# Where the weights and the activations of a two-layer trunk begin in a partition: multiples of 128 bytes for the one, 64 bytes past one for the other

## The chip, the core and the metric

The kernel runs on one core of a Trainium2 chip. The metric is the device time of one execution in microseconds, the median of several runs. The core has five engines that matter here: TensorE (PE in the profile; its weight loads are listed apart as PEld), VectorE (DVE), ScalarE (ACT), GpSimd (POOL) and SyncE (SP), which here only issues DMAs.

## The reference

Two layers of a hybrid trunk on 256 tokens of width 1024, all in 32-bit floats. A layer norms x, multiplies it with one wide input matrix, runs four branches of attention on the pieces, gates and adds their outputs, multiplies with an output matrix, and ends with an MLP with a squared ReLU:

```python
def hybrid_layer(x, ...):
    h = rms_norm(x, g_mix)
    (sb_q, sb_k, sb_v, gla_q, gla_k, gla_v, gla_lr, gla_r, dn_qkv, dn_a, dn_b, dn_gate,
     dil_q, dil_k, dil_v, gate_logits) = jnp.split(h @ w_in, IN_OFFSETS, axis=-1)
...
    gates = jax.nn.sigmoid(gate_logits.reshape(B, S, N_BRANCH, D_MODEL))
    merged = jnp.zeros_like(x)
    for n, o in enumerate((o_sb, o_gla, o_dn, o_dil)):
        merged = merged + gates[:, :, n] * (o.reshape(B, S, BRANCH_WIDTH) @ w_branch[n])
    x = x + merged @ w_out
    h = rms_norm(x, g_mlp)
    return x + jnp.square(jax.nn.relu(h @ w_mlp_in)) @ w_mlp_out
```

The four branches are stick-breaking attention, gated linear attention, a gated delta rule and dilated attention, four heads each. `w_in` is 1024 x 7448, `w_mlp_in` 1024 x 4096, `w_mlp_out` 4096 x 1024.

## The kernel before

All weights come as a stream of units of 128 x 2048 numbers, in the order in which they are used (`unit_list`): the pieces of `w_in`, each branch's gates and output matrix, `w_out` (`wo`), `w_mlp_in` (`mi`) and `w_mlp_out` (`mo`). A unit comes in two halves of 128 x 1024, each with one DMA into one of six `raw` buffers.

To keep the precision of 32 bits, every operand of a large product is split in two: a part that the engine's rounded 32-bit type (`float32r`) holds, and the rest. For weights ACT copies `raw` into `whi` and DVE subtracts, `wlo = raw - whi` (lines 247 and 248; five buffers each). Activations are split the same way: `ah`, `al` for the normed x, `oh`, `ol` for the output of a branch, `mh`, `ml` for the gated sum, `uh`, `ul` for the inside of the MLP. A large product is then three: high by high, high by low and low by high. A half of a unit is 24 of them.

Each of these is one weight load of 128 columns and one matmul that streams 256 columns. Mostly the weights are the loaded side and the activations the streamed one (`unit_F`, `units_out`); in the units whose result is wanted token by token (`unit_T`) the activations are loaded and the weights streamed. In the unit `mini` only 64 columns are loaded. All of them are issued by the helper at line 199.

Between the halves of units stands the small work of the branches, as threads that each go one step further at the end of a half; a table of pauses (`PAUSE`), written by hand, says how many halves lie between a step and the one that needs it on another engine. The order on each engine is the order in which the code issues.

Buffers of a partition are laid one behind the other, each at the next multiple of 32 bytes. A buffer whose size isn't a multiple of 128 bytes so shifts all that come after it: the constants `C` (1422 numbers), the parameters `PR` (2 x 433), `nea` (4) and the buffers `d6` (6 x 260) do.

Of the kernel before, what the change touches and what calls it, by code (L numbers as in the profile page):

```python
# [19 lines left out]
NL = 2  # L20
# [53 lines left out]
# columns of the packed parameters of a layer  # L74
P_GMIX, P_GMLP, P_CONV, P_DTB, P_ALOG, P_GLAB = 0, 8, 16, 40, 44, 48
P_GLAG, P_DNG, P_DILQ, P_DILK, P_LR2, NPAR = 49, 113, 177, 241, 305, 433
# columns of the constants
C_ID, C_NEGU, C_NEG1, C_UT, C_GT, C_STR, C_SBN, C_DIL = 0, 128, 256, 384, 512, 640, 768, 896
C_COS, C_SIN, C_SEL, C_S32, C_I32, C_H4, C_AB, NCON = 1280, 1312, 1344, 1346, 1378, 1410, 1414, 1422
LV = (1, 2, 4, 8, 16, 32, 64)  # L80

# [37 lines left out]
def lay_out(inp):  # L119
    a = {k: np.asarray(v) for k, v in inp.items()}  # L120
    w_in, w_br, w_out, w_mi, w_mo = (a[k] for k in ("w_in", "w_branch", "w_out", "w_mlp_in", "w_mlp_out"))
    W = np.zeros((len(UNITS), 128, 2048), np.float32)

    def kcols(w, c0, n=256):
        """[p][kt][column]"""
        return w[:, c0:c0 + n].reshape(8, 128, n).transpose(1, 0, 2).reshape(128, 8 * n)

    def fcols(w, c0):
        """[p][half of the columns][kt][column]"""
        return w[:, c0:c0 + 256].reshape(8, 128, 2, 128).transpose(1, 2, 0, 3).reshape(128, 2048)  # L130

    def krows(w, r0, halves=1):
        """[p][half of the columns][kt][column]"""
        n = 1024 // halves
        return w[r0:r0 + 256].reshape(2, 128, halves, n).transpose(1, 2, 0, 3).reshape(128, 2048)

    for n, (l, kind, arg) in enumerate(UNITS):
        if kind == "inF":
            W[n] = fcols(w_in[l], OFF[arg])
        elif kind == "inT":  # L140
            W[n] = kcols(w_in[l], OFF[arg])
        elif kind == "mini":
            m = np.zeros((1024, 32), np.float32)
            m[:, 0:8] = w_in[l][:, 2320:2328]
            m[:, 8:24] = w_in[l][:, 1280:1296]
            W[n][:, :256] = kcols(m, 0, 32)
        elif kind == "gate":
            W[n] = fcols(w_in[l], OFF["gates"] + arg[0] * 1024 + arg[1] * 256)
        elif kind == "br":
            W[n] = krows(w_br[l, arg], 0, 2)  # L150
        elif kind == "wo":
            W[n] = krows(w_out[l], arg * 256)
        elif kind == "mi":
            W[n] = fcols(w_mi[l], arg * 256)
        else:
            W[n] = krows(w_mo[l], arg * 256)
    P = np.zeros((NL, 128, NPAR), np.float32)
    for l in range(NL):
        P[l][:, P_GMIX:P_GMIX + 8] = a["norm_mix_g"][l].reshape(8, 128).T
        P[l][:, P_GMLP:P_GMLP + 8] = a["norm_mlp_g"][l].reshape(8, 128).T  # L160
        P[l][:, P_CONV:P_CONV + 24] = a["dn_conv_w"][l].reshape(6, 128, 4).transpose(1, 0, 2).reshape(128, 24)
        P[l][:, P_DTB:P_DTB + 4] = a["dn_dt_bias"][l][None]
        P[l][:, P_ALOG:P_ALOG + 4] = a["dn_a_log"][l][None]
        P[l][:, P_GLAB] = a["gla_b_lr"][l]
        P[l][:, P_GLAG:P_GLAG + 64] = a["gla_norm_g"][l][None]
        P[l][:, P_DNG:P_DNG + 64] = a["dn_norm_g"][l][None]
        P[l][:, P_DILQ:P_DILQ + 64] = a["dil_q_norm_g"][l][None]
        P[l][:, P_DILK:P_DILK + 64] = a["dil_k_norm_g"][l][None]
        for r in (8, 40):
            P[l][r:r + 16, P_LR2:P_LR2 + 128] = a["gla_w_lr2"][l]  # L170
    X = np.ascontiguousarray(a["x"].reshape(256, 8, 128).transpose(2, 1, 0).reshape(128, 2048))
    C, M = constants()
    return {"xin": X, "w": W, "par": P, "con": C, "msk": M}


@with_exitstack
def trunk(ctx: ExitStack, tc: tile.TileContext, xin, w, par, con, msk, out, dbg=None, nl=NL):
# [26 lines left out]
    # ---------------- constants and x  # L204
    C = cons.tile([128, NCON], F32, name="C")
    MK = cons.tile([128, 5 * 128], U8, name="MK")
    x = cons.tile([128, 8, 256], F32, name="x")
    PR = cons.tile([128, NL, NPAR], F32, name="PR")
# [18 lines left out]
    # ---------------- the stream of weights  # L227
# [22 lines left out]
    def split_upto(h):  # L250
        """h counts halves of units"""
        while state["split"] <= min(h, 2 * total - 1):
            k = state["split"]
            hi = wp.tile([128, 1024], F32R, name="whi", bufs=HALVES)
            lo = wp.tile([128, 1024], F32R, name="wlo", bufs=HALVES)
            splits[k] = (hi, lo)
            src = raws.pop(k)
            if wcols(k // 2) == 256:
                # both parts side by side
                src, both = r3(src[:, :128], 4), r3(hi[:, :256], 4)  # L260
                ACT.copy(both[:, :, 0:32], src)
                DVE.tensor_sub(both[:, :, 32:64], src, both[:, :, 0:32].bitcast(F32))
            elif k == 0:
                state["first"] = (src, hi, lo)
            else:
                n = 512 if k == 1 else 1024
                for c in range(0, 1024, n):
                    split_part(src, hi, lo, slice(c, c + n))
            state["split"] += 1
            dma_upto(k + RAW)  # L270
# [15 lines left out]
    nc.sync.dma_start(C[:, C_NEG1 + 128:], con[:, C_NEG1 + 128:])  # L286
# [4 lines left out]
    # ---------------- small helpers  # L291
    def rsqrt(v, n, name):
        """v: [128, n] in SBUF, > 0"""
# [7 lines left out]
    def pause(name):  # L301
        """slack between a step and the one that reads it on another engine, in halves of units"""
# [18 lines left out]
    def new_act():  # L321
        return (acts.tile([128, 8, 256], F32R, name="ah"), acts.tile([128, 8, 256], F32R, name="al"))

    class Norm:
        """x times the gain, feature-major and split; the root mean square is applied to what is made of it"""
# [28 lines left out]
        def rows(self):  # L354
            """1 / rms of each token, on every partition"""
# [9 lines left out]
        def scaled(self, t):  # L365
            """x over the root mean square"""
# [4 lines left out]
        def flip(self):  # L371
            """from here on what is made of it needs no scale"""
# [12 lines left out]
    def half(h, evac_first=False):  # L385
        """weights of half h of the current unit; the halves after it are begun"""
# [11 lines left out]
    def mmF(o, wh, wl, c, h, kts=8, new=False):  # L398
        """feature-major product: three passes; that over the operand split last comes last"""
# [8 lines left out]
    def unit_F(h, new=False):  # L408
        """yields after each half, then a bank [128, 2, 256], feature-major; new: h has only just been made"""
# [7 lines left out]
    def unit_T(h):  # L417
        """token-major, a bank [128, 2, 256]"""
# [12 lines left out]
    def unit_mini(h):  # L431
        """feature-major [64, 256]: by the high parts of the weights and, 32 rows on, by the low ones"""
# [14 lines left out]
    def units_out(h, units, nm):  # L447
        """feature-major products in four banks [128, 2, 256], added to x; the last unit goes by output"""
# [49 lines left out]
    # ---------------- one layer  # L498
    def layer(l, nm):
# [5 lines left out]
        with tc.tile_pool(name=f"mlp{l}", bufs=1) as mp:  # L505
            uh = mp.tile([128, 32, 256], F32R, name="uh")
            ul = mp.tile([128, 32, 256], F32R, name="ul")
# [22 lines left out]
    def mixing(l, pr, mp, nm):  # L530
# [7 lines left out]

        def split_pair(ps):
            pair = [mp.tile([128, 2, 256], F32R, name=n, bufs=2) for n in ("oh", "ol")]  # L540
# [3 lines left out]
        def to_feature(o, br, tag):  # L544
            """o: token-major [128, 2, 256] in SBUF -> split feature-major"""
# [7 lines left out]
        def head_rms(o, gs, br, tag, need=None):  # L553
            """o: [128, 2, 4, 64]; gs: silu of the gate times the gain"""
# [16 lines left out]
        # ---- gated delta rule: the gates and their decays  # L571
        def decay_chain():
            yield ("mini",)
            nea = sm.tile([128, 4], F32, name="nea")
# [24 lines left out]
            # rows and columns of the running sums of g  # L599
# [15 lines left out]
            got["E"] = E = T([6, 260], "d6", 3).rearrange("p a b -> p (a b)")[:, :1536].rearrange(  # L615
# [11 lines left out]
        # the products with the queries, and the values  # L627
# [33 lines left out]
        # ---- gated delta rule  # L661
        def dn_chain():
# [4 lines left out]
            pre = T([6, 260], "d6", 3)[:, :, :256]  # L667
# [38 lines left out]
            MT = T([6, 260], "d6", 3).rearrange("p a b -> p (a b)")[:, :1536].rearrange(  # L706
# [23 lines left out]
            # (I + M)^-1 transposed: blocks of 32 by substitution, all heads at once, then by doubling.  # L730
            # mc[j, (t, h), k]: the blocks of -M transposed
# [31 lines left out]
            def half_y(t, s):  # L763
                """levels 32 and 64: only the blocks below the diagonal"""
# [69 lines left out]
        # ---- stick breaking  # L834
# [54 lines left out]
        # ---- dilated  # L889
        def rope_chain():  # L890
            yield ("dil_q", "dil_k")
            qk = got["dil_qk"]                                  # [128, 16 (q/k, t, h), 64]
# [94 lines left out]
        # ---- gated linear attention  # L987
# [41 lines left out]
        def gla_chain():  # L1029
# [24 lines left out]
            # the diagonal and the pairs of level 1, a column of each for a head  # L1054
# [14 lines left out]
            # levels 16 to 2, two at a time; two heads at a time  # L1069
# [31 lines left out]
        # ---- threads of small work beside the weights  # L1101
        done = set()

        class Thread:
# [4 lines left out]
            def advance(self):  # L1109
                """one stage; False when it must wait or is over"""  # L1110
# [53 lines left out]
        cin = T([6, 260], "d6", 3)[:, :, :259]  # L1164
# [81 lines left out]
        def unit_br(n):  # L1246
# [9 lines left out]
            for fp in range(4):  # L1256
# [15 lines left out]
                if n == GLA:  # L1272
                    got["m"].append((mp.tile([128, 2, 256], F32R, name=f"mh{fp}", tag=("U", "T", "Y0", "Y1")[fp]),
                                     mp.tile([128, 2, 256], F32R, name=f"ml{fp}",
                                             tag=("Vs", "dlT0", "dlT1", "sbs")[fp])))
# [18 lines left out]
    with tc.tile_pool(name="boot", bufs=2) as bp:  # L1294
        # the tensor engine is brought to its full clock while the first loads are under way
# [42 lines left out]
```

## Time and profile before

| | |
|---|---|
| median of 3 runs | 933.5 us (933.41 to 936.74) |
| span of the profiled execution | 932.1 us |
| TensorE busy, matmuls and loads | 910.4 and 884.4 us |
| DVE, ACT, POOL busy | 630.8, 534.4, 143.8 us |
| weights and other data read | 147.5 MB, 159 GB/s over the span |

A matmul's time in the profile is that from its start to its modelled end; matmuls overlap, so the distance between the starts of two that follow each other is what the stream of products costs, and not the listed mean of one. A granted clock of 1 is the upper of TensorE's two levels, 2.4 GHz, and 0.5 the lower, 1.2 GHz.

### The profile page before, as it was taken

The page shows a single profiled execution, that of the slowest core. Times are in us where ns is not written, and L with a number is a line of the kernel's source. Part 1 is how long each engine was busy: PE and PEld are TensorE (multiplying, and loading weights), DVE is VectorE, ACT ScalarE, POOL GpSimd, SP SyncE. Part 2 cuts the span into 40 slices and gives each one's busy share as a digit, 9 for nine tenths or more (in the row PEclk, how much of TensorE's full clock was granted, in tenths as well). Part 3 has the DMA queues.
Part 4 walks back from the last instruction along what each step waited for, and adds up shares of the span by engine and source line. Part 5 has one row for each costly group of instructions (what it writes and reads, how often), then busy time and mean ns, then how long its engine had stood idle before and what let it go on. Part 6 is the DMA issues. An engine that isn't in the chain of part 4 may idle for free.

```text
span 932.1 us, 18924 instructions
## 1 busy us (share of the span) xinstructions
PE 910.4 (98%) x7678; PEld 884.4 (95%) x7678; DVE 630.8 (68%) x1242; ACT 534.4 (57%) x842; POOL 143.8 (15%) x148
## 2 busy tenths in 40 slices
PE   8999999999999999999989999999999999999998
PEld 6899999999998999999988999999999989999998
DVE  5959999429577676644489599984485867665442
ACT  5596758754554655543456876586545545654331
POOL 3524201113212000000042450013030120000000
PEclk7999999999999999999999999999999999999999
DMA  8544454433544556656444445444344535656551
GB/s 278 199 139 133 140 178 135 144 130 114 162 142 171 174 190 201 203 188 197 152 135 142 142 132 168 158 138 153 98 154 135 208 113 183 204 197 198 191 161 46
DMA packets 43430, 149.78 MB, mean 161 GB/s; under 512 B 4944, under 2 KB 7248, under 8 KB 43344
## 3 DMA queue, kind: packets, MB, share of 16 engines
q1 hardware_dynamic: 43056, 148.35, 48.8%
q8 instruction: 60, 0.98, 0.4%
q10 hardware_dynamic: 288, 0.23, 0.1%
q14 instruction: 26, 0.21, 0.1%
HBM read 147.51 MB, written 1.05 MB: 159 GB/s over the span
## 4 chain that ended last, share of the span: by engine, by line
PE 84%; DVE 8%; ACT 3%; POOL 2%; issue 1%; DMA 1%; SPq 0%; DVEq 0%; ACTq 0%
PE bg L199 55%; PE fa L199 14%; PE fb L199 14%; POOL s L369 2%; DVE al L339 2%; DVE wlo L248 2%; ACT whi L247 1%; DVE x L486 1%; DMA x<-xin 1%; POOL sbs L859 1%; DVE s L1082 0%; DVE ush L751 0%; DVE ush L749 0%; DVE s L1068 0%; PE fb L972 0%
## 5 line engine op out<-in xcount | busy, mean ns | idle before, releaser
L248 DVE TENSOR_TENSOR wlo<-raw,whi 128x1024 fp32r<-128x1024 f32 (+2 forms) x280 | 350.0, 1268 | 183.0 <-ACT whi L247 182.9
L247 ACT CAST whi<-raw 128x1024 fp32r<-128x1024 f32 (+2 forms) x280 | 283.8, 1034 | 117.9 <-PE bg L199 58.2
L199 PE MATMUL bg<-ah,whi 128*128 128x256 f32 x1232 | 315.2, 292 | 6.4 <-ACT ah L375 4.6
L199 PE MATMUL bg<-al,whi 128*128 128x256 f32 x1232 | 305.6, 289 | 6.2 <-DVE al L339 6.2
L199 PEld LDWEIGHTS bg<-ah,whi 128*128 128x128 f32 x1232 | 239.6, 194 | 13.3 <-ACT ah L375 6.6
L199 PEld LDWEIGHTS bg<-al,whi 128*128 128x128 f32 x1232 | 238.7, 196 | 7.6 <-DVE al L339 7.4
L199 PE MATMUL bg<-ah,wlo 128*128 128x256 f32 x1216 | 179.6, 286 | 1.5 <-DVE wlo L248 1.5
L199 PEld LDWEIGHTS bg<-ah,wlo 128*128 128x128 f32 x1216 | 162.5, 195 | 2.5 <-DVE wlo L248 2.5
L199 PE MATMUL fa<-uh,whi 128*128 128x256 f32 x256 | 70.4, 276 | 0.0
L199 PE MATMUL fa<-uh,wlo 128*128 128x256 f32 x256 | 70.4, 276 | 0.0
L199 PE MATMUL fa<-ul,whi 128*128 128x256 f32 x256 | 69.7, 276 | 0.0
L199 PE MATMUL fb<-uh,whi 128*128 128x256 f32 x224 | 61.6, 276 | 0.0
L199 PE MATMUL fb<-uh,wlo 128*128 128x256 f32 x224 | 61.6, 276 | 0.0
L199 PE MATMUL fb<-ul,whi 128*128 128x256 f32 x224 | 61.0, 276 | 0.0
L513 ACT ACTIVATE sq<-rl 128x512 f32<-128x512 f32 x32 | 20.2, 632 | 70.3 <-DVE rl L512 70.3
L445 DVE TENSOR_TENSOR ul<-sq,uh 128x512 fp32r<-128x512 f32 x32 | 22.2, 693 | 43.2 <-ACT uh L444 43.2
L1271 POOL TENSOR_TENSOR mg<-mg,gt 128x512 f32<-128x512 f32 x20 | 31.1, 1572 | 129.2 <-DVE gt L1270 129.2
L199 PEld LDWEIGHTS fa<-uh,whi 128*128 128x128 f32 x256 | 48.1, 188 | 0.0
L199 PEld LDWEIGHTS fa<-uh,wlo 128*128 128x128 f32 x256 | 48.1, 188 | 0.0
L199 PEld LDWEIGHTS fa<-ul,whi 128*128 128x128 f32 x256 | 47.6, 188 | 0.0
L199 PEld LDWEIGHTS fb<-uh,whi 128*128 128x128 f32 x224 | 42.1, 188 | 0.0
L199 PEld LDWEIGHTS fb<-uh,wlo 128*128 128x128 f32 x224 | 42.0, 188 | 0.0
(276 smaller groups left out, 1470.5 us busy)
## 6 DMA issues: line engine op xcount, KB each, us to landing
raw<-w SPq DMA_DIRECT2D x275, 512.0 KB, 4.3
x<-xin SPq DMA_DIRECT2D x3, 256.0 KB, 6.1
out_dram<-x SPq DMA_DIRECT2D x3, 256.0 KB, 2.1
C<-con SPq DMA_DIRECT2D x1, 519.0 KB, 6.9
raw<-w SPq DMA_DIRECT2D x4, 128.0 KB, 5.3
gt<-msk SPq DMA_DIRECT2D x2, 160.0 KB, 4.7
x<-xin SPq DMA_DIRECT2D x2, 128.0 KB, 2.8
raw<-w SPq DMA_DIRECT2D x4, 64.0 KB, 3.9
```

What stands on the lines that cost most here:

```text
L199: PE.matmul(o, l, r, start=start, stop=stop, skip_group_check=True)
L247: ACT.copy(hi[:, c], src[:, c])
L248: DVE.tensor_sub(lo[:, c], src[:, c], hi[:, c].bitcast(F32))
L339: DVE.scalar_tensor_tensor(self.h[1][:, kt, :], x[:, kt, :], self.g[:, kt:kt + 1], self.h[0][:, kt, :].bitcast(F32), op0=OP.mult, op1=OP.s ...
L369: POOL.tensor_tensor(t[:, kt, :], x[:, kt, :], self.R, op=OP.mult)
L445: DVE.tensor_sub(lo, src, hi.bitcast(F32))
L486: DVE.tensor_add(xs, pairs[fp], xs)
L513: ACT.activation(sq, rl, AF.Square)
L859: POOL.tensor_tensor(sp[:, :, c:c + 128], sp[:, :, c:c + 128], over(STR, 2), op=OP.mult)
L1271: (DVE if n == GLA and MADD[fp] else POOL).tensor_tensor(m, m, g, op=OP.add)
```

## The change

No instruction is added, removed or moved: on each engine the same instructions stand in the same order and wait for the same semaphores. Only addresses change. Buffers whose size is not a multiple of 128 bytes are widened to one (`whole`), and the activations' buffers are made 128 bytes longer and used from their 17th number on (`shifted`). So that all of it fits, the scratch at the start of each partition that is kept for DMAs with descriptors made by software shrinks from 16384 to 4096 bytes.

Where an operand begins in its partition, in bytes past a multiple of 128 (slices in a buffer are whole multiples of 512 bytes, so this holds for all of them):

| buffers | before | after |
|---|---|---|
| `raw`, `whi`, `wlo` (weights) | 96 | 0 |
| `ah`, `al` | 96 | 64 |
| `oh`, `ol` and `mh`, `ml` | 64 | 64 |
| `uh`, `ul` | 32 | 64 |
| constants `C` | 0 | 0 |
| `x`, `PR` | 64 | 0 |
| most tiles of the branches | 64, some 0, 32 or 96 | 0 |

The diff, without the comments that it also drops:

```diff
+def whole(n):
+
+    return -(-n // 32) * 32
+
+
+def shifted(tile, n, by=16):
+
+    return tile[:, by:by + n]
...
-    C = cons.tile([128, NCON], F32, name="C")
+
+    C = cons.tile([128, whole(NCON)], F32, name="C")
...
-    PR = cons.tile([128, NL, NPAR], F32, name="PR")
+    PR = cons.tile([128, whole(NL * NPAR)], F32, name="PR")[:, :NL * NPAR].rearrange("p (l c) -> p l c", l=NL)
...
-    nc.sync.dma_start(C[:, C_NEG1 + 128:], con[:, C_NEG1 + 128:])
+    nc.sync.dma_start(C[:, C_NEG1 + 128:NCON], con[:, C_NEG1 + 128:])
...
     def new_act():
-        return (acts.tile([128, 8, 256], F32R, name="ah"), acts.tile([128, 8, 256], F32R, name="al"))
+        return tuple(r3(shifted(acts.tile([128, 2080], F32R, name=n), 2048), 8) for n in ("ah", "al"))
...
-            uh = mp.tile([128, 32, 256], F32R, name="uh")
-            ul = mp.tile([128, 32, 256], F32R, name="ul")
+            uh, ul = (r3(shifted(mp.tile([128, 8224], F32R, name=n), 8192), 32) for n in ("uh", "ul"))
...
+        def d6():
+            return T([whole(6 * 260)], "d6", 3)
+
         def split_pair(ps):
-            pair = [mp.tile([128, 2, 256], F32R, name=n, bufs=2) for n in ("oh", "ol")]
+            pair = [r3(shifted(mp.tile([128, 544], F32R, name=n, bufs=2), 512), 2) for n in ("oh", "ol")]
...
-            nea = sm.tile([128, 4], F32, name="nea")
+            nea = sm.tile([128, 16], F32, name="nea")[:, 0:4]
...
-        cin = T([6, 260], "d6", 3)[:, :, :259]
+        cin = r3(d6()[:, :1560], 6)[:, :, :259]
...
-                    got["m"].append((mp.tile([128, 2, 256], F32R, name=f"mh{fp}", tag=("U", "T", "Y0", "Y1")[fp]),
-                                     mp.tile([128, 2, 256], F32R, name=f"ml{fp}",
-                                             tag=("Vs", "dlT0", "dlT1", "sbs")[fp])))
+                    got["m"].append(tuple(
+                        r3(shifted(mp.tile([128, 544], F32R, name=f"{n}{fp}", tag=tags[fp]), 512), 2)
+                        for n, tags in (("mh", ("U", "T", "Y0", "Y1")), ("ml", ("Vs", "dlT0", "dlT1", "sbs")))))
...
-    nc = _bacc.Bacc("TRN2", target_bir_lowering=False, num_devices=1)
+    nc = _bacc.Bacc("TRN2", target_bir_lowering=False, num_devices=1, dynamic_dma_scratch_size=4096)
```

The other three uses of `d6` (`E`, `MT` and `pre`) are rewritten in the same way as `cin`.

## Rows read from the trace of the kernel before

**Rows 1.** The page: span, and busy time, share and instructions of each engine.
```profile
span 932.1 us, 18924 instructions
PE 910.4 (98%) x7678; PEld 884.4 (95%) x7678; DVE 630.8 (68%) x1242; ACT 534.4 (57%) x842; POOL 143.8 (15%) x148
```
**Rows 2.** The page: granted TensorE clock in 40 slices, in tenths (9 is 90% up).
```profile
PEclk7999999999999999999999999999999999999999
```
**Rows 3.** Timeline of PE, first MLP product: start us, us, engine, line, operation, out<-in.
```profile
319.88 0.28 PE L199 MATMUL bg<-ah,whi 128*128 128x256 f32 x1
...
320.84 0.28 PE L199 MATMUL bg<-ah,whi 128*128 128x256 f32 x1
```
**Rows 4.** The chain that ended last, second MLP product: start us, us, what.
```profile
387.02 1.36 PE fb L199 x12
388.38 1.36 PE fa L199 x12
```
**Rows 5.** The same chain, product with `w_out`.
```profile
266.07 1.42 PE fa L199 x12
267.49 1.42 PE fb L199 x12
```
**Rows 6.** Groups of matmuls: count | busy us, mean ns of one | idle before.
```profile
L199 PE MATMUL bg<-ah,whi 128*128 128x256 f32 x1232 | 315.2, 292 | 6.4 <-ACT ah L375 4.6 <-ACT whi L247 1.8
L199 PE MATMUL bg<-al,whi 128*128 128x256 f32 x1232 | 305.6, 289 | 6.2 <-DVE al L339 6.2
...
L199 PE MATMUL bg<-ah,wlo 128*128 128x256 f32 x1216 | 179.6, 286 | 1.5 <-DVE wlo L248 1.5
...
L199 PE MATMUL bg<-oh,whi 128*128 128x256 f32 x128 | 35.3, 296 | 1.1 <-DVE gt L1270 1.1
...
L199 PE MATMUL bg<-whi,ah 128*128 128x256 f32 x224 | 32.7, 288 | 0.0
...
L199 PE MATMUL fa<-mh,whi 128*128 128x256 f32 x64 | 17.8, 282 | 0.0
```
**Rows 7.** Timeline of PE in the unit `mini`, loads of 64 columns.
```profile
26.86 0.28 PE L199 MATMUL bg<-ah,whi 128*64 128x256 f32 x1
...
28.00 0.28 PE L199 MATMUL bg<-ah,whi 128*64 128x256 f32 x1
```
**Rows 8.** Timeline of PEld: eight loads whose matmuls stream 4 columns.
```profile
195.29 0.97 PEld L199 LDWEIGHTS fb<-C,dlT 128*128 128x128 f32 x8
```
**Rows 9.** Groups of weight loads, 128 and 64 columns.
```profile
L199 PEld LDWEIGHTS fa<-C,Y 128*128 128x128 f32 x32 | 3.7, 192 | 0.0
...
L199 PEld LDWEIGHTS fa<-U,Y 64*64 64x64 f32 x32 | 2.2, 134 | 0.5
```
**Rows 10.** Busy us in stretches: PE, PEld, DVE, ACT, POOL, then clock, DMA, GB/s.
```profile
100.00:120.00 20.00, 19.89 (x170) 19.20 (x169) 19.07 (x70) 14.52 (x19) 0.00 (x0) 1.00 0.50 162
120.00:140.00 20.00, 20.00 (x157) 18.95 (x157) 18.39 (x78) 9.96 (x22) 0.00 (x0) 1.00 0.52 164
140.00:160.00 20.00, 20.00 (x171) 19.52 (x171) 19.63 (x91) 16.25 (x28) 3.36 (x4) 1.00 0.40 126
...
293.00:381.00 88.00, 88.00 (x724) 87.95 (x723) 57.49 (x65) 48.01 (x62) 0.00 (x0) 0.98 0.57 186
...
470.00:506.00 36.00, 31.64 (x218) 29.41 (x217) 30.13 (x47) 19.02 (x39) 15.89 (x15) 0.91 0.41 133
...
560.00:600.00 40.00, 39.98 (x326) 38.25 (x325) 37.48 (x145) 24.21 (x40) 0.00 (x0) 1.00 0.49 159
```
**Rows 11.** Groups: DVE's subtraction of 128x512 for `ul`.
```profile
L445 DVE TENSOR_TENSOR ul<-sq,uh 128x512 fp32r<-128x512 f32 x32 | 22.2, 693 | 43.2 <-ACT uh L444 43.2
```
**Rows 12.** The instructions of tile `ml`: min/median/max ns of one.
```profile
L1237 DVE TENSOR_TENSOR ml<-mg,mh x8: 675/688/693, 262.9 to 728.2; 128x512 fp32r<-128x512 f32 x8
```
**Rows 13.** Waits: who waited for whom, us in total, times, longest.
```profile
DVE wlo L248 <- ACT whi L247: 182.9, 139, 6.5
...
PE bg L199 <- DVE al L339: 6.2, 6, 1.0
```
**Rows 14.** The page's DMA queues: kind, packets, MB, share of 16 engines.
```profile
q1 hardware_dynamic: 43056, 148.35, 48.8%
q8 instruction: 60, 0.98, 0.4%
```

More of the change, by code (lines that the diff above doesn't have):

```diff
@@ L614, in decay_chain @@
             yield from pause("e10")
-            got["E"] = E = T([6, 260], "d6", 3).rearrange("p a b -> p (a b)")[:, :1536].rearrange(
+            got["E"] = E = d6()[:, :1536].rearrange(
                 "p (a h c) -> p a h c", a=3, h=4)
@@ L666, in dn_chain @@
             cw = pr[:, P_CONV:P_CONV + 24]
-            pre = T([6, 260], "d6", 3)[:, :, :256]
+            pre = r3(d6()[:, :1560], 6)[:, :, :256]
             for b in range(6):
@@ L705, in dn_chain @@
             yield from pause("d13")
-            MT = T([6, 260], "d6", 3).rearrange("p a b -> p (a b)")[:, :1536].rearrange(
+            MT = d6()[:, :1536].rearrange(
                 "p (a h c) -> p a h c", a=3, h=4)
```

## The prediction

> **What bounds the kernel now.** I read the busy line first. The matmul row of TensorE is busy 910.4 of 932.1 us, DVE 630.8, ACT 534.4 [rows 1], and the granted clock stands at its upper level nearly everywhere [rows 2]. A busy matmul row alone proves little, since matmuls overlap; so I looked at how far apart their starts are, in the timeline of TensorE. From here I call that distance the pitch. It should be the same for all the large products: each loads 128 columns and streams 256 columns, and 256 columns at 2.4 GHz take 106.7 ns. It is not the same:
>
> - activations `ah`, `al` against weights `whi`, `wlo`: eight steps from 319.88 to 320.84 us, 120 ns each [rows 3];
> - activations `uh`, `ul` against the same weights: twelve in 1.36 us, 113.3 ns [rows 4];
> - activations `mh`, `ml`: twelve in 1.42 us, 118.3 ns [rows 5].
>
> The clock is at its upper level in all three, the instruction is the same, the weights lie in the same buffers, and no wait stands between. What differs is where the activations begin. By the table of positions ahead, weights are at 96 (bytes past a multiple of 128, which I call the phase), `ah` and `al` at 96, `uh` and `ul` at 32, `mh`, `ml`, `oh`, `ol` at 64. So the distance between the phases is 0, 64 and 32 bytes, and the pitch is 120, 113.3 and 118.3 ns: it falls as the distance grows. My reading is that the weight load of the next matmul, which runs beside the streaming of this one, meets it in the memory when both are at one phase.
>
> The rest of the page says that the pitch is worth time: TensorE waits for almost nothing (the longest wait in total is 6.2 us, for `al`), while DVE waits 182.9 us in total for ACT [rows 13]. The next engine is DVE, close behind in parts of the attention stage: 19.07, 18.39 and 19.63 of 20 us, and 37.48 of 40 in the second layer [rows 10].
>
> **The change part by part.** No engine's instructions change in number, order or waits; only addresses do.
>
> *Products with `ah` and `al`.* Phases 96 and 96 become 64 and 0 (or 0 and 64 where the activation is the loaded side). The page counts 1232 + 1232 + 1216 with the weights loaded and 3 x 224 with the activations loaded [rows 6], 4352 in all; 32 of them load only 64 columns (the unit `mini`), which leaves 4320. The nearest row with a distance of 64 bytes is that of `uh`: 113.3 ns [rows 4]. 4320 x (120.0 - 113.3) = 28.9 us.
>
> *Products with `oh`, `ol`, `mh`, `ml`.* Distance 32 becomes 64. 3 x 128 with `oh`, `ol` and 2 x 3 x 64 with `mh`, `ml` [rows 6] make 768; 768 x (118.3 - 113.3) = 3.8 us.
>
> *Products with `uh`, `ul`.* Distance 64 stays; the phases go from 96 and 32 to 0 and 64. Sixteen units of two halves, eight columns of tiles, three products, two layers: 1536. By the distance alone they gain nothing.
>
> *Does beginning on a multiple of 64 bring more than the distance?* The trace has no pair of 0 and 64, so I bound it. From above: 113.3. From below: eight weight loads of 128 columns whose matmuls stream only 4 columns start (0.97 - 0.19) / 7 = 0.111 us apart, one of them taking 192 ns [rows 8, 9]. There the load alone sets the pace; a load of 64 columns takes 134 ns, so the columns are what it pays for. A product that must load 128 new columns each time will hardly go under 111.4 ns. The products of `mini`, which load half as many columns at phases 96 and 96, go at 1.14 us for ten steps, 114 ns [rows 7]: with half the load the collision is almost gone, and what is left is again about 113. I take 113.3, the row with the same distance, and keep 111.4 for the range: 1.9 x 6624 = 12.6 us more.
>
> The Trainium skill ("TensorE: Matmul & The Clock Gate", Part 2, step 1) speaks against the change: TensorE has two independent read ports into SBUF, and loading the next weights takes no read bandwidth from the running matmul. By that rule phases could not matter, and the time would stay at 933.5. This case's trace disagrees: 120 against 113.3 ns for one and the same instruction.
>
> *The small products* (transposes, chunks of the branches) get phase 0 on both sides in most cases, where many had 64 on both. Equal stays equal; a few transposes that meet the constants lose their distance, some 100 of them by about 10 ns at the most: 1 us, inside the bounds.
>
> *DVE, ACT and DMA.* Their operands move too. The same subtraction of 128x512 takes 693 ns with tiles at phase 32 and 688 with tiles at 64 [rows 11, 12], so a phase costs them nothing that I can see. The scratch that shrinks to 4096 bytes serves a kind of queue that this kernel has not: the page lists hardware queues and instruction queues only [rows 14]. Nothing.
>
> *What the gain meets.* 32.7 us disappear from TensorE only where it is the bound. In the first product of the MLP it surely is: 88 of 88 us busy, DVE 57.49 [rows 10]; 1536 of the 4320 products lie there and in its twin, 10.3 us. In the attention stage a stretch of 20 us with some 170 products shrinks by up to 1.1 us, while DVE has 0.93, 1.61 and 0.37 us to spare, and 2.52 in 40. So DVE stays just under the bound but for the stretch from 140 us, short by 0.8; twice, for two layers: 1.5 us. Where a layer begins, TensorE waits for the norm (31.64 of 36 us busy from 470 us [rows 10]); what its 218 products save there, 1.5 us, is mostly given back, and likewise at the start: 2.5 us. Together 4 us are lost.
>
> **Sum.** The profiled span is 932.1 us; the median of the runs is 933.5, 1.4 us more for what lies around the span. 933.5 - 28.9 - 3.8 + 4 = 904.8.
>
> **The rivals.**
>
> *Alignment counts as well.* The load alone sets the pace, 111.4 ns for all 6624 products. For it: the row of loads is at phase 64, on a multiple of 64, and all present large products have a side at 32 or 96. Against: in [rows 4] nothing shows what the last 2 ns are. 12.6 us more off TensorE, of which DVE takes back about a third: 896.
>
> *Only the streaming counts* and the load hides: 106.7 ns. For it: 256 columns need no more. Against: the row of loads, 111.4 [rows 8]. 6.6 x 6624 = 43.7 us more, a third given back: 876. The Trainium skill (the same page, "Back-to-back issue gap") gives 262 cycles for 256 columns, which is 109 ns; by it the sum would be an estimated 886. No product here goes at that pace.
>
> *DVE becomes the bound.* Of the gain, 2784 x 6.7 + 3.8 = 22.5 us lie in the attention stage, where each chain of small steps hands work between DVE, ACT and TensorE with slack counted in halves of weights, and these halves get shorter. If half of it is lost in waits of TensorE for DVE: 912 to 916. For it: 19.63 of 20 us. Against: DVE itself waits 182.9 us for ACT's copies, whose pace follows the buffers that TensorE frees.
>
> *The change does nothing to the pitch*: it hangs on something that goes with the stage, not on the phase (the banks written, the units' order). Against: `mh` and `uh` products have the same loop and differ. 933.5.
>
> *Slower: the phase of the streamed side decides, not the distance.* Streamed at 32 the pitch is 113.3, at 64 it is 118.3, at 96 it is 120. If 64 is simply a bad phase, `uh` and `ul` lose what they have now: 1536 x (118.3 - 113.3) = 7.7 us, and `ah` gains 4320 x 1.7 = 7.3; and if with a load at 0 all went at 120, the loss would be 1536 x 6.7 + 768 x 1.7 = 11.6 us: 945. It decides from a pitch of about 119 for `uh`. Against: where activations are loaded at 96 and weights streamed at 96, the pitch is that of equal phases too.
>
> **How the numbers follow.** 113.3 ns, 904.8 us: 0.50. 111.4 ns, 896: 0.22. 106.7 ns, 876: 0.05. DVE bound, 914: 0.12. No change: 0.07. Slower, 945: 0.04. The range from 887 to 917 takes in the first, second and fourth with some room on both sides; the third, fifth and sixth stay out. Faster by over 0.5% (about what a measurement of this kernel can tell from no change): 0.50 + 0.22 + 0.05 + 0.12 = 0.89; within: 0.07; slower: 0.04.
>
> **What would show it.** In the timeline of after, products with `ah` 113 ns apart (eight steps in 0.91 us, not 0.96), twelve `mh` products in 1.36 us, `uh` unchanged at 1.36. Each MLP's first product shorter by 5.1 us. DVE's busy time as before, its waits for ACT shorter, TensorE's waits for `wlo` and the chains longer by a few us. The forecast is wrong if `ah` stays at 120, if `uh` moves by more than 2 ns, or if waits of TensorE grow by over 10 us.

## The result

The changed kernel takes 927.0 us where the kernel before took 933.7 in the same runs (medians of 12 runs each). The ratio is 0.9929, with an interval from 0.9913 to 0.9946: some 0.7% faster. The forecast was 904.8 us and its range ended at 887; the time lies 10 us above the upper end, 917.

The page after, span, TensorE's and the other engines' busy time, and the granted clock (of before: [rows 1, 2]):

```profile
span 923.0 us, 18924 instructions
PE 898.1 (97%) x7678; PEld 871.4 (94%) x7678; DVE 630.3 (68%) x1242; ACT 534.2 (58%) x842; POOL 144.3 (16%) x148
PEclk8999999999999999999999999999999999999999
```

DVE, ACT and POOL do what they did. What changed is TensorE's pitch, the distance between the starts of two large products. Timeline of PE in the first MLP product after (eight steps), to be held against [rows 3]:

```profile
316.67 0.28 PE L209 MATMUL bg<-ah,whi 128*128 128x256 f32 x1
...
317.61 0.28 PE L209 MATMUL bg<-ah,whi 128*128 128x256 f32 x1
```

Eight steps in 0.94 us, 117.5 ns: better than 120, but far from 113.3. The chain of the second MLP product and of the product with `w_out` after, against [rows 4] and [rows 5]:

```profile
266.12 1.41 PE fa L209 x12
...
400.48 1.41 PE fa L209 x12
401.89 1.40 PE fb L209 x12
```

Here is the surprise: twelve products with `uh` took 1.36 us before and now take 1.41. Products with `mh` went from 1.42 to 1.41 only. Waits hardly moved, against [rows 13]:

```profile
DVE wlo L258 <- ACT whi L257: 183.2, 135, 6.4
...
PE bg L209 <- DVE al L349: 6.2, 6, 1.0
```

TensorE issues the same 7678 matmuls, small ones included, in the same order in both traces, so they can be paired one by one. Taking the distance from each large product's start to the next one's where nothing interrupts it (under 135 ns in both):

| products | pairs | before, ns | after, ns | sum, us |
|---|---|---|---|---|
| `ah`, `al` streamed, weights loaded | 3421 | 119.8 | 117.4 | -8.1 |
| `ah`, `al` loaded, weights streamed | 640 | 119.8 | 114.9 | -3.1 |
| `oh`, `ol` | 342 | 118.3 | 115.2 | -1.0 |
| `mh`, `ml` | 383 | 118.3 | 117.4 | -0.4 |
| `uh`, `ul` | 1535 | 113.4 | 117.0 | +5.6 |
| sum of the pitch | | | | -7.0 |

The time follows this sum, but two more things go into it. The two profiled spans differ by 9.1 us: 7.0 of pitch and 5.3 of clock (in the one of after 145 products ran at the lower clock's pitch, in the one of before 198), of which pauses and small products give back about 3. So pitch less what is given back is worth some 4 us. The granted clock also varies between runs of one kernel, and comparing at one clock gives nearly that: at a mean of 0.983 three runs of after took 928.0 to 929.1 us and nine of the kernel before, taken beside the experiments, 932.8 to 934.5 (4.4 between the medians); at 0.987 three took 925.6 to 926.4 and six 929.7 to 930.9 (4.8). The rest of the 6.7 us between the medians goes with the higher clock that the runs of after got; whether that was chance or a consequence of the change isn't shown.

### The profile page after: what moved, and what is told of

It reads as the page before. It is cut to its first block, busy times and chain, and to the rows that moved or that the text cites. A ratio compares the mean times of both kernels' runs of the same rounds, so it can differ in the third digit from the quotient of the medians.

```text
span 923.0 us, 18924 instructions
## 1 busy us (share of the span) xinstructions
PE 898.1 (97%) x7678; PEld 871.4 (94%) x7678; DVE 630.3 (68%) x1242; ACT 534.2 (58%) x842; POOL 144.3 (16%) x148
## 3 DMA queue, kind: packets, MB, share of 16 engines
q1 hardware_dynamic: 43056, 148.35, 49.7%
## 4 chain that ended last, share of the span: by engine, by line
PE 73%; DVE 14%; ACT 7%; POOL 2%; issue 2%; DMA 0%; SPq 0%; DVEq 0%
PE bg L209 45%; PE fa L209 14%; PE fb L209 13%; DVE wlo L258 4%; ACT whi L257 2%; DVE al L349 2%; POOL sbs L871 1%; POOL s L379 1%; DVE d L685 1%; DVE ush L763 1%; DVE x L496 1%; ACT d L631 1%; DVE ush L761 1%; DVE Y L765 1%; DVE s L1094 0%
## 5 line engine op out<-in xcount | busy, mean ns | idle before, releaser
L209 PE MATMUL bg<-ah,whi 128*128 128x256 f32 x1232 | 307.4, 288 | 5.7 <-ACT ah L385 4.4
L209 PE MATMUL bg<-al,whi 128*128 128x256 f32 x1232 | 297.1, 283 | 6.2 <-DVE al L349 6.2
L209 PEld LDWEIGHTS bg<-ah,whi 128*128 128x128 f32 x1232 | 233.8, 190 | 12.7 <-ACT ah L385 6.6
L209 PEld LDWEIGHTS bg<-al,whi 128*128 128x128 f32 x1232 | 233.0, 191 | 7.8 <-DVE al L349 7.4
L209 PE MATMUL bg<-ah,wlo 128*128 128x256 f32 x1216 | 175.7, 282 | 2.8 <-DVE wlo L258 2.8
L209 PEld LDWEIGHTS bg<-ah,wlo 128*128 128x128 f32 x1216 | 157.9, 189 | 3.7 <-DVE wlo L258 3.7
```

Source lines behind the costliest of these rows:

```text
L209: PE.matmul(o, l, r, start=start, stop=stop, skip_group_check=True)
```

## The experiments

**A map of the pitch, and three other pairs of phases.** `m1_grid` leaves out the whole computation, as do all kernels called "TensorE alone" below; TensorE alone runs rows of 32 products, each row with one of eight places for the loaded side (`wa` to `wh`: 0, 32, ... 224 bytes past a multiple of 256) and one of eight for the streamed (`ma` to `mh`), and one sum is the output:

```python
def run(m, s, n, b):
    for i in range(n):
        PE.matmul(bk[b][:, 0:256], ws[s][:, 128 * (i % 4):128 * (i % 4) + 128],
                  ms[m][:, 256 * (i // 4 % 2):256 * (i // 4 % 2) + 256], start=i == 0, stop=i == n - 1, ...)
...
for s in range(8):
    for m in range(8):
        run(m, s, 32, m % 2)
```

> Leaves out the whole computation: only TensorE works, on a stream of loads of 128 columns and matmuls of 256 columns, 32 for each pair of phases in which the loaded and the streamed side begin (0, 32, 64, 96, 128, 160, 192, 224 bytes past a multiple of 256, each with each); the output is one of the sums. Theory H (half-lines: a distance of 64 bytes is good only where both sides begin 32 bytes off a multiple of 64): 120 ns for every pair at distance 0, 113.3 for 96 with 32 and 32 with 96, about 117 for 0 with 64 and 64 with 0. Theory M (the streamed side's phase alone decides): about 115 for every pair that streams at 0, 113.3 at 32, 117 to 118 at 64, 120 at 96, whatever the loaded side's phase. If phases are not the cause at all: one pitch for all 64 pairs.

The timeline of `m1_grid`; a row's pitch is (time - 0.28) / 31. The first seven rows have the loaded side at 0 and the streamed at 32, 64, ... 224; in the last both are at 32:

```profile
23.40 3.94 PE L210 MATMUL bg<-mb,wa 128*128 128x256 f32 x32
27.18 3.93 PE L210 MATMUL bg<-mc,wa 128*128 128x256 f32 x32
30.95 3.99 PE L210 MATMUL bg<-md,wa 128*128 128x256 f32 x32
34.77 3.96 PE L210 MATMUL bg<-me,wa 128*128 128x256 f32 x32
38.57 3.92 PE L210 MATMUL bg<-mf,wa 128*128 128x256 f32 x32
42.33 3.81 PE L210 MATMUL bg<-mg,wa 128*128 128x256 f32 x32
45.98 3.94 PE L210 MATMUL bg<-mh,wa 128*128 128x256 f32 x32
...
53.54 4.00 PE L210 MATMUL bg<-mb,wb 128*128 128x256 f32 x32
```

118.1, 117.7, 119.7, 118.7, 117.4, 113.9, 118.1 and 120.0 ns. The rows at 64 and at 192 differ, though both are 64 modulo 128: **the distance counts modulo 256**, streamed minus loaded. With the loaded side at other places the same distances give the same pitch, but for five rows of 64: two at a distance of 192 took 117.8, one at 64 took 113, one at 160 took 118.7 and one at 32 took 117. Both theories fell.

This map fits before at once. Modulo 256 the weights lay at 224, `ah` and `al` at 224 (distance 0: 120), `uh` and `ul` at 160 (192: 113.3), `mh` and `oh` at 192 (224: 118.3). After, weights lie at 128, `ah` and `uh` at 192, `al` and `ul` at 64: a buffer of 2080 numbers is 32.5 times 256 bytes, so the next one lands 128 further on. The distances are now 64 for products that stream `ah` or `uh` and 192 for those that stream `al` or `ul`, and against `whi` the two come in turn. (`oh`, `ol` and `mh`, `ml` lie at 64 or at 192 past a multiple of 256 from buffer to buffer; a branch's `oh` and `ol` have the same.)

Beside it ran the changed kernel with all phases turned, by a pad ahead of the buffers (`e1_96_32`: 24 numbers; `e2_32_96`: 8), and with the activations' shift taken away (`e3_0_0`):

```diff
+    cons.tile([128, 24], F32, name="pad")
...
-def shifted(tile, n, by=16):
+def shifted(tile, n, by=0):
```

> The changed kernel with 96 bytes of padding ahead of the weights: weights at phase 96, all activations at 32, the pair at which uh had 113.3 ns before. H: 113.3 ns everywhere, about 905 us. M: 113.3 where activations are streamed, 120 in the units that load activations and stream weights (672 products, 4.5 us more): about 909 us. If the change's pitch of 117 has another cause than phases: about 927 us as after.

> The changed kernel with 32 bytes of padding ahead of the weights: weights at phase 32, all activations at 96. H: 113.3 ns everywhere, about 905 us. M: 120 where activations are streamed (as ah before), 113.3 where weights are streamed: about 941 us.

> The changed kernel without the shift of the activations: both sides at phase 0. H, and my first theory of the distance: 120 ns everywhere, about 945 us. M: 115 ns everywhere, about 915 us.

`e1_96_32` took 925.95 us (ratio 0.9919, from 0.9890 to 0.9948), `e2_32_96` 929.1 in its one run, `e3_0_0` 934.9, with 933.4 for the kernel before beside them. Turning all phases changes nothing: products with `uh` at 117.0 ns in the first two as after. In `e3_0_0` the distance is 0 modulo 128 everywhere, but 0 and 128 in turn modulo 256, and the pitch is not 120 but 118.7 for `ah` and 117.8 for `uh`; in the sum of the pitch that is 3.2 us more than before. The chain of `e3_0_0`, `mh` and then `uh`:

```profile
263.92 1.42 PE fa L209 x12
...
401.22 1.41 PE fa L209 x12
```

**Is it the alternation?** `m2_steps` (TensorE alone, the loaded side at 0) runs rows of 48 at distances in steps of 16 bytes, up and down, then 192 and 64 in turn within a row. `e4_192` and `e5_64` give high and low parts the same distance in the layer: buffers are multiples of 256 bytes, the activations 192 or 64 past one:

```diff
-    return -(-n // 32) * 32
+    return -(-n // 64) * 64
...
-def shifted(tile, n, by=16):
+def shifted(tile, n, by=48):
...
-        return tuple(r3(shifted(acts.tile([128, 2080], F32R, name=n), 2048), 8) for n in ("ah", "al"))
+        return tuple(r3(shifted(acts.tile([128, 2112], F32R, name=n), 2048), 8) for n in ("ah", "al"))
```

> Leaves out the whole computation: TensorE alone, as in m1_grid, with the loaded side always at a multiple of 256 bytes. First the streamed side at 0, 16, 32 ... 240 bytes past one, 48 matmuls each, then the same backwards; then 96 matmuls each with streamed sides that change from one to the next: 192 always, 64 always, 192 and 64 in turn, 64 and 192 in turn, 192, 64 always; then three in turn (a, b, a) as in the kernel's triples. Theory L (the pitch is set by the distance of the streamed from the loaded side modulo 256, and by whether it stays the same from one matmul to the next): 113.3 ns at 192, 117.8 at 64, 120 at 0 both ways, and 117 or more wherever 64 and 192 alternate. Theory P (at 64 and at 192 two rhythms are possible, and the one in which the row is entered stays): 113.3 or 117.8 at both, not the same upwards and downwards. If alternation does nothing: the mean of the two, 115.6.

> The changed kernel with all buffers at multiples of 256 bytes and the activations 192 bytes past one, high and low parts alike (in the changed kernel ah and uh are 64, al and ul 192 bytes past the weights modulo 256). L: 113.3 ns wherever activations are streamed, 113.3 to 118 in the units that load them; about 905 us, at most 909. P: part of the products at 113.3, part at 117.8, between 905 and 925. If the alternation of the parts is not the cause: 117 as in after, about 927.

> As e4_192, but the activations 64 bytes past a multiple of 256, high and low alike. L: 117.8 ns where activations are streamed, 113.3 to 114 in the units that load them; about 928 us. P: 113.3 or 117.8, between 905 and 928. If only the distance modulo 128 and the constancy count: 905, the same as e4_192.

The timeline of `m2_steps`: distances 64, 112 and 192 (`me`, `mh`, `mm`), 192 and 64 held for 96 products, and twenty products with the two in turn:

```profile
42.63 5.82 PE L213 MATMUL bg<-me,wt 128*128 128x256 f32 x48
...
59.80 5.60 PE L213 MATMUL bg<-mh,wt 128*128 128x256 f32 x48
...
87.97 5.62 PE L213 MATMUL bg<-mm,wt 128*128 128x256 f32 x48
...
201.02 11.06 PE L213 MATMUL bg<-mm,wt 128*128 128x256 f32 x96
211.92 11.47 PE L213 MATMUL bg<-me,wt 128*128 128x256 f32 x96
...
223.34 0.28 PE L213 MATMUL bg<-me,wt 128*128 128x256 f32 x1
...
225.68 0.28 PE L213 MATMUL bg<-me,wt 128*128 128x256 f32 x1
```

Held at 192: (11.06 - 0.28) / 95 = 113.5 ns; held at 64: 117.8; in turn: 2.34 / 20 = 117.0, as in the layer after (117.0 to 117.5). So the change put its products on a mixture whose quick part doesn't come through. But holding the distance at 192 was not the cure: `e4_192` took 926.3 us (0.9917, from 0.9897 to 0.9938), `e5_64` 930.5 (0.9970, from 0.9942 to 0.9997). Theory L fell. The chain of `e4_192`, a stretch with `mh` and one with `uh`, at one and the same distance:

```profile
262.98 1.36 PE fa L209 x12
...
400.45 1.41 PE fa L209 x12
```

Within a stretch the pitch is 113.3 or 117.8 and stays so: at 117.8, for instance, for all products of the MLP's second part. At 192 there are **two rhythms**, as theory P said; what decides between them is the next question.

**Which distance is quick however it begins?** `m3_entries` (TensorE alone) gives each of 30 distances ten beginnings: an odd matmul of 8 to 232 columns ahead of the row of 28 (eight of them), or a wait for DVE (two):

```python
if cols:
    PE.matmul(b[:, 256:256 + cols], wt[:, 0:128], ms[:, d:d + cols], start=True, stop=True, ...)
for i in range(n):
    o = d + 256 * (i // 4 % 2)
    PE.matmul(b[:, 0:256], wt[:, 128 * (i % 4):128 * (i % 4) + 128], ms[:, o:o + 256], ...)
```

`e6_112` is `e4_192` with the activations 112 bytes past a multiple of 256 (`by=28`).

> Leaves out the whole computation: TensorE alone. For each of 30 distances of the streamed from the loaded side (modulo 256) ten stretches of 28 matmuls, eight of them entered by one odd matmul of 8 to 232 columns that shifts the rhythm, two after a wait for DVE. Theory R (two rhythms at a distance of 64 or 192, and the entry decides which): at 64 and 192 some entries give 113.3 and some 117.8 ns, and each stays to the stretch's end; at 112 all give 113.3; at 0 all give 120. Theory A (the pitch belongs to the distance alone, and what disturbs it in the whole kernel is the other engines' traffic): one pitch for each distance, whatever the entry: 113.3 at 192 and 112, 117.8 at 64.

> As e4_192, but the activations 112 bytes past a multiple of 256, the other distance at which TensorE alone went at 113.3 ns both upwards and downwards. R: one rhythm, 113.3 ns wherever activations are streamed, 117 to 119 in the units that load them (distance 144): about 908 us, at most 912. A: the whole kernel's traffic disturbs this distance as it does 192: a mixture, 920 to 930 us.

The mean of a row's last 15 products: at a distance of 0 all ten rows took 119.9 to 120.1 ns, at 64 all 117.7 to 117.9, at 112 all 113.3 to 113.7; at 192 five took 113.2 to 113.4 and five 117.6 to 117.8. So theory R held, but not at 64, where it expected two rhythms. The last products of two rows at 192, timeline of `m3_entries`:

```profile
870.54 1.86 PE L209 MATMUL even<-ms,wt 128*128 128x256 f32 x15
...
874.11 1.70 PE L209 MATMUL even<-ms,wt 128*128 128x256 f32 x13
```

(1.86 - 0.28) / 14 = 113 and (1.70 - 0.28) / 12 = 118 ns. The two rows differ only in the odd matmul ahead, 8 columns or 40: how a row begins decides its rhythm. At 16 the ten rows took anything from 113 to 120. And a row at 112 is quick only after up to fourteen products at some 118, which is the price of its beginning.

`e6_112` took 919.0 us (0.9867, from 0.9820 to 0.9913). Theory R had the pitch right and the time too low (912 at the most): against before the sum of the pitch falls by 22.3 us, but pauses and small products grow by some 5. Chain in the second MLP product, and timeline of the units that load activations:

```profile
400.40 1.36 PE fb L209 x12
```

```profile
52.47 1.12 PE L209 MATMUL bg<-whi,al 128*128 128x256 f32 x8
53.43 1.13 PE L209 MATMUL bg<-wlo,ah 128*128 128x256 f32 x8
```

The first is back at 113.3; products with `ah` and `al` streamed come to 114.0 with what each beginning costs. In the units with the sides swapped the distance is -112, that is 144, and (1.12 - 0.28) / 7 = 120 ns.

**The swapped units, first try.** `e7_112_both` moves the weights that those units stream so that their distance is 112 as well:

```diff
-            hi = wp.tile([128, 1024], F32R, name="whi", bufs=HALVES)
-            lo = wp.tile([128, 1024], F32R, name="wlo", bufs=HALVES)
+            by = 56 if UNITS[k // 2][1] == "inT" else 0
+            hi, lo = (shifted(wp.tile([128, 1088], F32R, name=n, bufs=HALVES), 1024, by) for n in ("whi", "wlo"))
```

> As e6_112, and the weights that the units with token-major outputs read begin 224 bytes further on, so that streamed minus loaded is 112 modulo 256 there as well as in the other units. Theory R (the pitch goes by that distance modulo 256, and 112 is a distance at which every entry falls into the quick rhythm): those units go from 120 to 113.3 ns, some 650 products x 6.7 ns = 4.4 us under e6_112, so about 914.6 us. Rival W (TensorE's gain there is swallowed by waits for VectorE and ScalarE, as part of it was in e6_112): the products take 113.3 ns, the time stays at 918 to 919 us.

> TensorE alone, no part of the layer: rows of products at each of the 64 distances 0, 4, ... 252 bytes (streamed minus loaded, modulo 256), five entries each (8, 72 or 168 columns in the odd product ahead, or a wait for VectorE). Theory R: 112 gives 113.3 to 113.4 ns at all entries, 64 gives 117.8 at all, 0 gives 120 at all, 192 gives 113.4 or 117.8 by the entry; no distance goes under 113.3. Rival F (113.3 isn't a floor): one or more distances go to 111.4, the pitch of the loads alone.

A miss: 918.4 us (0.9837, from 0.9795 to 0.9879), and the swapped units stay where they were, timeline of `e7_112_both`:

```profile
52.27 1.12 PE L209 MATMUL bg<-whi,ah 128*128 128x256 f32 x8
```

So the distance is not all. `m4_all` (TensorE alone, the loaded side at 0, all 64 distances) was right on 0, 112 and 192 (four of five beginnings quick) and nearly so on 64 (one of five at 113.4), and showed no row under 113.3 at any distance; the slowest were at 4 and 244, 123 ns.

**Both sides' places.** `m5_grid16` (TensorE alone) runs all 256 pairs of places in steps of 16 bytes, with two beginnings each.

> TensorE alone, no part of the layer: loaded and streamed side each at all sixteen phases 0, 16, ... 240 modulo 256, 256 pairs, 28 products a row, two entries each. In e7_112_both the units that load activations (loaded 112, streamed 224) kept 119.7 ns at a distance of 112. Theory A (the loaded side's own place counts beside the distance): 113.4 ns at distance 112 where the loaded side lies at 0, 64, 128 or 192, and more, 120 at (112, 224) among them, where it lies between these. Theory D (the distance alone counts, and what kept those units at 120 lies in the kernel around them): 113.4 ns at distance 112 for all sixteen places of the loaded side.

Timeline of `m5_grid16`, the last 13 products of three rows: (0, 112), (112, 48) and (112, 224), the loaded side first:

```profile
73.05 1.64 PE L209 MATMUL odd<-ms,wt 128*128 128x256 f32 x13
```

```profile
862.23 1.64 PE L209 MATMUL odd<-ms,wt 128*128 128x256 f32 x13
```

```profile
942.45 1.72 PE L209 MATMUL even<-ms,wt 128*128 128x256 f32 x13
```

113.3, 113.3 and 120 ns (at the other beginning the third pair took 116.7). Over all pairs, by the mean of a row's last 15 products, of 16 rows each:

| loaded side | distance 112: rows at 113.3 to 113.4 | distance 192: rows at 113.3 to 113.4 |
|---|---|---|
| at a multiple of 32 | 16 (none slower) | 10 (the others near 117.8) |
| 16 past one | 0 (116.6 to 120) | 16 (none slower) |

Theory D fell. Theory A was right that the loaded side's own place counts and gave 120 at (112, 224), but the border is 32, not 64. Elsewhere only two more distances had any quick row: 16 (3 of 16, loaded side at a multiple of 32) and 64 (2 of 16, loaded side 16 past one).

**The swapped units, second try.** Their loaded side lies at 112, which is 16 past a multiple of 32; so `e8_112_48` gives them a distance of 192, with `by = 12` in place of 56.

> As e7_112_both, and the weights that the units with token-major outputs stream begin 48 instead of 224 bytes past a multiple of 256. Loaded 112, streamed 48: distance 192. Theory A2 (read from m5_grid16: with the loaded side at a multiple of 32 the sure distance is 112, with the loaded side 16 past one it is 192): those units' products go from 119.7 to 113.3 ns, 640 products x 6.4 ns = 4.1 us of TensorE's time, so about 914.5 us where e7_112_both took 918.4. Rival W (the gain is swallowed by waits for VectorE and ScalarE): products at 113.3 ns, the time at 918. Rival D (it was not the place of the loaded side that kept them at 120): 119.7 ns again and 918.

914.0 us (0.9771, from 0.9744 to 0.9799), 2.3% faster than the kernel before, and within 1 us of what theory A2 said. (Of the 4.4 us under `e7_112_both` the pitch of the swapped units makes 3.7.) Timeline of the swapped units, and the page:

```profile
52.47 1.07 PE L209 MATMUL bg<-whi,al 128*128 128x256 f32 x8
53.37 1.07 PE L209 MATMUL bg<-wlo,ah 128*128 128x256 f32 x8
```

```profile
span 912.6 us, 18924 instructions
PE 886.2 (97%) x7678; PEld 859.3 (94%) x7678; DVE 629.8 (69%) x1242; ACT 534.4 (59%) x842; POOL 143.5 (16%) x148
```

(1.07 - 0.28) / 7 = 113 ns. This is the best version found; it changes no instruction either.

## Why the prediction was wrong

**TensorE's pitch is the bound, and operands' places set it: right.** Before, after and `e8_112_48` have the same instructions but for their addresses, and the time follows the pitch, less what waits and small products give back: 7.0 us of pitch and 4 to 5 of time at an equal clock after, 26.4 and 20 in `e8_112_48` (at 0.983 one run of 913.6, at 0.987 two of 910.9). The rival "no change to the pitch" fell with the table above.

**The term for `ah` and `al`, 4320 x 6.7 = 28.9 us: this step failed.** It took the price of `uh` for "a distance of 64 bytes", with phases taken modulo 128. The three rows that it stood on ([rows 3 to 5]) fit that reading and fit the right one, distances of 0, 192 and 224 modulo 256, equally well; nothing in the trace of before could tell 64 from 192. Measured, the term is 8.1 + 3.1 = 11.2 us: with the weights loaded, two thirds of the products (those that stream `ah`) got 64, a distance at 117.8, and the 192 of the other third brings nothing when the two come in turn (117.0 in `m2_steps`). In the swapped units it is `ah` that has 192, two thirds of the products, each held for eight in a row; there the quick rhythm shows, 114.9 in the mean. Timeline after:

```profile
53.50 1.07 PE L209 MATMUL bg<-whi,ah 128*128 128x256 f32 x8
```

**`uh` and `ul` unchanged: failed by the same step**, with the other sign. They had a distance of 192 before, in its quick rhythm, and the change took that away: +5.6 us. And 113.3 was the price of one of two rhythms, not of the distance, which three rows could not show: in `e4_192` the same products at the same distance take 117.8. The forecast itself had named a move of `uh` by over 2 ns as its refutation. The rival on the slow side had this loss (7.7 us for `uh` against 7.3 gained for `ah`) and had the mechanism wrong: it is not the streamed side's phase, since `e1_96_32` with the streamed side at 32 and 160 pays the same.

**`oh`, `ol`, `mh`, `ml`, 3.8 us: too large for the same reason**; measured 1.0 + 0.4.

**113.3 as the price, and no more from alignment: right.** Phases 0 and 64, which the trace of before had not, are no better than others, and 64 distances in `m4_all` and 256 pairs in `m5_grid16` give nothing under 113.3. The rivals with 111.4 and 106.7 ns fell, and so did DVE as the bound: after, TensorE's waits are nearly those of before. The Trainium skill ("TensorE: Matmul & The Clock Gate", Part 2, step 1) says that loading the next weights takes no read bandwidth from the running matmul. The 113.3 to 123 ns measured for one instruction by its operands' places show that how the two sides lie to each other counts all the same; whether read bandwidth is what they share, no run here shows.

**DVE, ACT and DMA at nothing: right.** 630.8 and 534.4 us busy before, 630.3 and 534.2 after; the DMA queue's packets take 48.8% before and 49.7% after.

**4 us lost to waits: about right in size, wrong in place.** It was priced for a gain of 32.7 us; `e8_112_48`, with 26.4, is nearest to that. Pauses between large products that are not the clock's grow there from 24.6 to 29.1 us in the sum, and small products take 1.7 more. In the stretch that the prediction named, from 140 us, nothing is lost: DVE is at 19.98 of 20 us, but TensorE at 20.00. It loses where the prediction saw DVE just under the bound, between 100 and 120 us. Windows of `e8_112_48` (columns as in [rows 10]), the wait in the first of them, and the sum of such waits:

```profile
100.00:120.00 20.00, 18.38 (x162) 17.99 (x159) 19.22 (x65) 13.81 (x18) 0.00 (x0) 1.00 0.52 173
140.00:160.00 20.00, 20.00 (x179) 19.53 (x178) 19.98 (x88) 17.39 (x28) 3.62 (x4) 1.00 0.45 148
```

```profile
110.63 0.39 PE L209 MATMUL bg<-ol,whi 128*128 128x256 f32 x1 [1.62 <-DVE ol L456]
```

```profile
PE bg L209 <- DVE ol L456: 3.2, 2, 1.6
```

TensorE waits 1.6 us in each layer for `ol` from DVE, for which it hardly waited before: there it was busy 19.89 of the 20 us.

What stays open: why the places act so, and what in a beginning picks the rhythm at 192. The runs give the map, not its cause.

## What to carry to other kernels

Three rows can fit two moduli: before pricing a change by where operands lie, write their addresses modulo 256 at least, for every copy of a buffer, since a length that is no multiple of 256 makes neighbours drift, and ask which other modulus fits the same rows. A kernel of TensorE alone with a row of products per pair of places measures the whole map in one run, beginnings included. For products that load 128 and stream 256 four-byte columns, a streamed side 112 bytes past the loaded one (loaded at a multiple of 32), or 192 past it (loaded 16 past such a multiple), was quick at every beginning tried: two for each of eight places of the loaded side, and ten more for 112 with the loaded side at 0.

## What the runs showed of the hardware

- The pitch of one and the same product runs from 113.3 to 123 ns by the two places modulo 256.
- One distance can have two rhythms, 113.3 and 117.8 ns; a matmul of 40 columns in place of 8 ahead of the row switches between them, and a rhythm once taken is kept for hundreds of products (117.8 through the MLP's second part in `e4_192`, 768 products).
- A mixture of a quick and a slow distance in turn goes nearly at the pace of the slow one (117.0 of 113.5 and 117.8).
- After TensorE has waited for a layer's norm, its products run at the lower clock for a while. In `e6_112` it waits 1.03 us for `al` and starts again at 286.48 us; from 288.14 nine steps take 1.92 us, 213 ns, and later nine take 1.04, 116 ns; the row of windows within the first (columns as in [rows 10]) gives a granted clock of 0.50, the lower level, with TensorE busy throughout:

```profile
288.14 0.41 PE L209 MATMUL bg<-ah,whi 128*128 128x256 f32 x1
...
290.06 0.41 PE L209 MATMUL bg<-al,whi 128*128 128x256 f32 x1
...
293.06 0.28 PE L209 MATMUL bg<-al,whi 128*128 128x256 f32 x1
...
294.10 1.07 PE L209 MATMUL bg<-ah,wlo 128*128 128x256 f32 x8
```

```profile
288.00:290.00 2.00, 2.00 (x11) 2.00 (x11) 2.00 (x3) 0.19 (x1) 0.00 (x0) 0.50 0.34 119
```

  How many products fall into such stretches ranges from 145 to 211 in the profiles of these kernels, and the 66 between make some 7 us of span; so pitches are compared product by product, and times at an equal clock or by medians.
